# A whole transformer block on one core: inputs modulated straight from PSUM, token loads in one queue, decays behind the norms, and another order into and out of the expert loop

## The chip, the cores and the metric

One of the eight cores of a Trainium2 chip runs the program. The metric is the device time of one execution in microseconds (us), as the median of several runs. The engines named below are PE (matrix products), DVE and ACT (vector work), POOL (vector work and gathers) and SP (starts transfers). PSUM is the memory into which PE writes, SBUF the one from which it reads.

## The reference, cut to what matters

```python
h    = modulate(rmsnorm(x, g_mix), sh1, sc1)          # 512 tokens; hc likewise for 256 context tokens
proj = h @ w_in                                       # pools, q, k, v, gates, merge gates
y    = bidir_retention(q, k, v, log_sigmoid(decay), s_f, s_b)
x    = x + g1 * mix_tokens(proj, y)
hf   = modulate(rmsnorm(x, g_ffn), sh2, sc2)
# expert layer: 8 heads each choose 16 of 16384 single-neuron experts per token
g, eidx = softmax(top16), indices                     # from two top-16 lists of 128 keys
act  = gelu(einsum('thkd,td->thk', u[eidx], hf))
x    = x + g2 * einsum('thk,thkd->td', g * act, v[eidx])
out  = rmsnorm(x, final_g)
```

`modulate(h, shift, scale)` is `h * (1 + scale) + shift`; shift and scale come from products of `silu(c)` with `ada_w`.

## The kernel before, in words

Products with full float32 accuracy are made as three products of rounded parts (`mm3`): an operand is split into `hi` (a cast, on ACT, L164 or L146) and `lo` (value minus `hi`, on DVE, L169 or L147). Weights land in `raw` tiles (three buffers) and are split the same way. The order of the instructions on each engine is set by a scheduler from the order of the code, the buffers of the pools and its own estimates; each engine then runs its list strictly in order.

**The front** (`front`, `mods`). Six blocks of 128 tokens (two of context, four of x) are loaded as `xb`, alternately by SP and by ACT. `decays` computes log-sigmoid of eight decay rates with an Exp and a chain of tiny DVE operations; nothing in `mods` needs its result, the attention behind it does. ACT squares the six blocks (L299), a Sqrt makes the factors `rs`, and DVE and ACT scale the blocks. `shift_scale(i)` makes shift and scale of the two column groups k = 2i and 2i+1: one row block `ada0` through PE (L321), one `ada1` through DVE (L326, multiply and sum over `crow`, twice), then a few small operations up to `m` (L341), with two PSUM buffers of the tag U. `transpose(range(8))` turns all 48 blocks of 128x128 by PE (L362) and ACT copies them to `xT` in SBUF (L363). `modulate(i)` applies scale and shift to `xT`, ACT for the context and DVE for x, and splits the result into `hc` and `hx`. `project(i)` multiplies these by the first weights: for each k six products of 256 columns (`hc`) and twelve of 512 (`hx`).

**The experts.** All 16384 experts are computed densely for three of the four token blocks (384 tokens, `NB` = 3), 128 groups of 128 experts: `up` makes `a = gelu(u . hfT)`, in two halves each (`run_up(n)` runs n halves), `weigh` multiplies `a` by the routing weights `G` (L1173) and splits it to `ph` and `pl`, `down` adds `a . v` into six PSUM banks `Y`. The fourth block is computed by gathers on POOL and sums on DVE (`acc`). 31 groups (`AHEAD`) are taken up ahead, before `Y` exists.

The routing weights are made in **the hot loop**: for 24 sets of 16 tokens DVE writes one-hot matrices (`onehots`, L1100 to L1103), PE multiplies them (L1115), ACT writes the product from PSUM into `st` (L1116), and a transfer takes `st` to `gd` in memory. Up halves fill the loop. `prep(n)` splits the group n of u. Behind the loop come two `prep`, the first two loads of v, the reads of `G` (`read`), and steps of the top-k selection for the fourth block (`tick`, some 30 small DVE operations each, with POOL between them), then `weigh(0)`, the last up halves, and the dense loop over j: weigh(j+1), split of v, `down(j)`, one `up` in three of four steps.

**The tail.** The last `LAST` = 4 groups run down block by block. `finish` (L1038 to L1047) multiplies by `g2`, adds x, squares on ACT, normalizes and stores, for the gathered block (`f0`, started inside the loop as soon as all gathers are summed) and for the three of `Y`.

## Time and profile before

| | |
|---|---|
| median of 3 runs | 1787.21 us (1786.79 to 1787.54) |
| the profiled execution | 1787.09 us, of which its span is 1785.3 us |
| busy in the span | PE 1725.4 us, DVE 1328.0 us, ACT 777.2 us, POOL 357.8 us |
| mean granted clock of PE | 0.987 of 2.4 GHz |

The span is what the profile covers; 1.8 us lie outside it. Busy shares are means over stages with different limits, so the sections below go by stage: the front up to 72 us, attention and the rest up to 670 us, the hot loop to 800 us, the hand-over from it to the dense loop to 840 us, the dense loop, and the tail from 1755 us.

### The profile page before, as it was taken

What the parts mean: (1) busy time and instruction counts of PE and PEld (TensorE: products, weight loads), DVE (VectorE), ACT (ScalarE), POOL (GpSimd) and SP (SyncE); (2) the same over time, 40 slices, a digit from 0 to 9 for tenths busy, and PEclk for the clock granted to TensorE, in tenths of its full rate; (3) what the DMA queues carried; (4) which work ended last, traced back from release to release, by engine and by line L of the source; (5) the groups of instructions that cost most, each with busy time, mean ns of one, the idle gap of its engine ahead of it and who ended that gap; (6) DMA issues with size and microseconds to landing.
All of it is one profiled execution on the core that took longest, in us unless ns stands there. A gap on an engine that the chain in (4) does not pass through costs nothing.

```text
span 1785.3 us, 26030 instructions
## 1 busy us (share of the span) xinstructions
PE 1725.4 (97%) x9882; PEld 1552.6 (87%) x9882; DVE 1328.0 (74%) x2408; ACT 777.2 (44%) x1320; POOL 357.8 (20%) x385
## 2 busy tenths in 40 slices
PE   6999999999989998997999999999999999999997
PEld 4899988888989997986889989999899998999995
DVE  7766365664468999988947788877888777888766
ACT  7443345222344347893344344443444434444343
POOL 0222230000026840004421111221111211212100
PEclk9999999999999999998999999999999999999999
DMA  8211134675332225774569989989899899989952
GB/s 321 101 48 48 60 124 128 214 250 182 111 138 77 95 81 192 273 286 143 162 239 360 334 310 321 328 308 343 309 319 331 317 333 319 315 324 314 345 188 106
DMA packets 134190, 406.13 MB, mean 227 GB/s; under 512 B 10896, under 2 KB 60336, under 8 KB 114480
## 3 DMA queue, kind: packets, MB, share of 16 engines
q1 hardware_dynamic: 111744, 243.50, 40.7%
q0 software_dynamic: 18432, 134.23, 20.1%
q10 hardware_dynamic: 3888, 26.74, 3.6%
q8 instruction: 77, 1.26, 0.3%
q14 instruction: 49, 0.40, 0.1%
HBM read 375.05 MB, written 29.38 MB: 227 GB/s over the span
## 4 chain that ended last, share of the span: by engine, by line
PE 81%; DVE 11%; issue 2%; ACT 2%; DMA 1%; POOL 0%; DVEq 0%; ACTq 0%; SPq 0%; POOLq 0%
PE ps L154 17%; PE ps L152 17%; PE ps L153 17%; PE Y L153 9%; PE Y L154 9%; PE Y L152 9%; DVE o L1103 3%; DVE lo L169 2%; DVE eq L1100 2%; PE ps L805 1%; DVE o L1101 1%; ACT hi L164 1%; DMA keys<-keys 0%; DMA raw<-uvd 0%; PE ps L693 0%
## 5 line engine op out<-in xcount | busy, mean ns | idle before, releaser
L169 DVE TENSOR_TENSOR lo<-raw,hi 128x1024 fp32r<-128x1024 f32 x297 | 365.3, 1231 | 79.9 <-ACT hi L164 77.0
L164 ACT CAST hi<-raw 128x1024 fp32r<-128x1024 f32 x332 | 343.4, 1050 | 179.0 <-DMA raw<-uvd 96.0
L152 PE MATMUL ps<-hfT,hi 128*128 128x384 f32 x1120 | 383.4, 342 | 11.8 <-ACT hi L164 10.4
L154 PE MATMUL ps<-hfT,lo 128*128 128x384 f32 x1120 | 381.7, 341 | 10.7 <-DVE lo L169 10.7
L153 PE MATMUL ps<-hfT,hi 128*128 128x384 f32 x1120 | 379.7, 339 | 1.6 <-DVE hfT L147 1.6
L152 PE MATMUL Y<-hi,ph 128*128 128x512 f32 x768 | 299.6, 390 | 3.5 <-ACT ph L146 3.0
L153 PE MATMUL Y<-lo,ph 128*128 128x512 f32 x768 | 301.5, 393 | 0.6 <-DVE lo L169 0.5
L154 PE MATMUL Y<-hi,pl 128*128 128x512 f32 x768 | 301.6, 393 | 0.1
L1011 POOL DMA_INDIRECT uv<-uv,eidx x128 | 154.3, 1206 | 638.5 <-DVE acc L1030 601.0
L152 PEld LDWEIGHTS ps<-hfT,hi 128*128 128x128 f32 x1120 | 213.8, 191 | 16.8 <-ACT hi L164 11.4
L154 PEld LDWEIGHTS ps<-hfT,lo 128*128 128x128 f32 x1120 | 213.7, 191 | 14.2 <-DVE lo L169 14.2
L153 PEld LDWEIGHTS ps<-hfT,hi 128*128 128x128 f32 x1120 | 214.1, 191 | 5.8 <-DVE hfT L147 2.0
L1138 ACT ACTIVATE a<-ps 128x384 f32<-128x384 f32 x128 | 62.9, 491 | 315.2 <-PE ps L154 311.9
L147 DVE TENSOR_TENSOR pl<-a,ph 128x384 fp32r<-128x384 f32 x128 | 70.9, 554 | 148.7 <-ACT ph L146 148.5
L152 PEld LDWEIGHTS Y<-hi,ph 128*128 128x128 f32 x768 | 144.5, 188 | 32.3 <-ACT ph L146 3.4
L154 PEld LDWEIGHTS Y<-hi,pl 128*128 128x128 f32 x768 | 144.5, 188 | 31.4 <-DVE pl L147 1.1
L153 PEld LDWEIGHTS Y<-lo,ph 128*128 128x128 f32 x768 | 144.4, 188 | 29.8 <-DVE lo L169 1.4
L1030 DVE SCALAR_TENSOR_TENSOR acc<-uv,act,acc 128x1024 f32<-128x1024 f32 x127 | 162.5, 1280 | 5.1
L1019 DVE SCALAR_TENSOR_TENSOR uv<-uv,hf 128x1024 f32<-128x1024 f32 x128 | 154.4, 1218 | 0.0
L169 POOL TENSOR_TENSOR lo<-raw,hi 128x1024 fp32r<-128x1024 f32 x35 | 85.5, 2451 | 236.7 <-ACT hi L164 226.6
L1116 ACT ACTIVATE st<-ps 128x512 f32<-128x512 f32 x96 | 91.4, 1115 | 9.7 <-PE ps L1115 8.3
L1021 ACT ACTIVATE act<-act 128x1 f32<-128x1 f32 x128 | 25.7, 201 | 145.7 <-DVE uv L1019 145.7
(287 smaller groups left out, 2870.8 us busy)
## 6 DMA issues: line engine op xcount, KB each, us to landing
raw<-uvd SPq DMA_DIRECT2D x252, 512.0 KB, 6.2
ada<-ada SPq DMA_DIRECT2D x48, 512.0 KB, 4.7
gd<-st ACTq DMA_DIRECT2D x24, 1024.0 KB, 4.8
raw<-w_in SPq DMA_DIRECT2D x44, 512.0 KB, 4.3
G<-gd SPq DMA_DIRECT2D x85, 256.0 KB, 7.0
raw<-wq SPq DMA_DIRECT2D x16, 512.0 KB, 3.9
raw<-ret_out SPq DMA_DIRECT2D x8, 512.0 KB, 4.8
raw<-w_out SPq DMA_DIRECT2D x8, 512.0 KB, 3.7
```

The lines of the kernel that those rows point to most:

```text
L147: (eng_lo or nc.vector).tensor_tensor(lo, src, hi.bitcast(F32), ALU.subtract)
L152: mm(out, a[0], b[0], start=first, stop=False)
L153: mm(out, a[0], b[1], start=False, stop=False)
L154: mm(out, a[1], b[0], start=False, stop=last)
L164: self.nc.scalar.copy(hi, raw)
L169: eng.tensor_tensor(lo, raw, hi.bitcast(F32), ALU.subtract)
L1011: self.nc.gpsimd.indirect_dma_start(out=t, out_offset=None, in_=self.I["uv"], in_offset=bass.IndirectOffsetOnAxis(ap=self.eidx[:, s:s + 1] ...
L1019: nc.vector.scalar_tensor_tensor(t[:, :D], t[:, :D], 1.0, self.hf, ALU.mult, ALU.mult, accum_out=act[:, 0:1])
L1030: nc.vector.scalar_tensor_tensor(self.acc, t[:, D:], act[:, 1:2], self.acc, ALU.mult, ALU.add)
L1103: nc.vector.tensor_tensor(wide(o2[:, r]), wide(eq), tokens(self.gq[:, r]), ALU.mult)
L1116: nc.scalar.mul(st[:, :, t:t + 4].rearrange("p m t -> p t m"), ps, 1.0 / GSCALE)
L1138: nc.scalar.activation(a, ps[:, :N], AF.Gelu)
```

## The change

1. `decays` runs behind the Sqrt step of the norms instead of ahead of `mods`.
2. All six token blocks are loaded by SP.
3. The 48 turned blocks are no longer made in one go and copied by ACT; `modulate(i)` turns the twelve that it needs into a U buffer, and its scale and shift read PSUM.
4. One up half moves from `routes` to the end of `heads`.
5. The write of `st` runs through the same elements in another order: before, it read PSUM in rows of 512 contiguous values and wrote values 64 bytes apart; now it writes four contiguous values (16 bytes) at a time and reads values 512 bytes apart.
6. The up halves of the hot loop come ahead of the one-hots of the next set, and there are 33 instead of 32 (4 in the first step, then 1, 1, 1 and from then on 2 in every third); the `prep` of two groups moves from behind the loop into its last two steps, and that of the last group ahead of `weigh(0)`. The load of v group 1 goes behind the reads of `G`.
7. The last groups are weighed up to three ahead, in ring buffers; `f0` starts behind the loop; the last downs run half by half; `finish` multiplies and adds per half.

```diff
@@ front
-            self.decays(hp)
+            self.hp = hp
...
@@ mods
-                (nc.scalar if b % 2 else nc.sync).dma_start(
+                nc.sync.dma_start(
                     xb, I["ctx"][b * P:(b + 1) * P] if b < 2 else I["x"][(b - 2) * P:(b - 1) * P])
...
             self.rstd(rs, ss, 1.0 / D)
+            self.decays(self.hp)
...
             def modulate(i):
+
                 for k in (2 * i, 2 * i + 1):
-                    for src, h, v in ((0, hcx, 1), (2, hx, 0)):
-                        n = h[0].shape[2]
-                        t = xT[:, k, src * P:src * P + n]
+                    for src, n, h, v in ((0, 2, hcx, 1), (2, 4, hx, 0)):
+                        pt = self.ps("U")
+                        for b in range(n):
+                            nc.tensor.transpose(pt[:, b * P:(b + 1) * P], xs[src + b][:, k * P:(k + 1) * P], self.ident)
+                        t = xT[:, k, src * P:(src + n) * P]
                         m, c = m1[:, 1, k, v:v + 1], m1[:, 0, k, v:v + 1]
                         if v:
-                            nc.scalar.activation(t, t, AF.Identity, scale=m, bias=c)
+                            nc.scalar.activation(t, pt[:, :n * P], AF.Identity, scale=m, bias=c)
                         else:
-                            nc.vector.tensor_scalar(t, t, m, c, ALU.mult, ALU.add)
+                            nc.vector.tensor_scalar(t, pt[:, :n * P], m, c, ALU.mult, ALU.add)
                         self.split(t, h[0][:, k], h[1][:, k])
-
-            def transpose(ks):
-                for k in ks:
-                    for b0, n in ((0, 2), (2, 4)):
-                        pt = self.ps()
-                        for b in range(n):
-                            nc.tensor.transpose(pt[:, b * P:(b + 1) * P], xs[b0 + b][:, k * P:(k + 1) * P], self.ident)
-                        nc.scalar.copy(xT[:, k, b0 * P:(b0 + n) * P], pt[:, :n * P])
...
             shift_scale(0)
-            transpose(range(8))
             modulate(0)
@@ heads, routes
-        self.run_up(5)
+        self.run_up(6)
...
-        self.run_up(3)
+        self.run_up(2)
@@ finish
-        for s, src in zip(S, parts):
+        for i, (s, src) in enumerate(zip(S, parts)):
             nc.vector.tensor_tensor(o[:, s], src, g2[:, s], ALU.mult)
-        for i, s in enumerate(S):
             nc.vector.tensor_tensor(o[:, s], o[:, s], x[:, s], ALU.add)
@@ weights
-            nc.scalar.mul(st[:, :, t:t + 4].rearrange("p m t -> p t m"), ps, 1.0 / GSCALE)
+            nc.scalar.mul(st[:, :, t:t + 4], ps.rearrange("p t m -> p m t"), 1.0 / GSCALE)
@@ experts
-            if j < P - LAST:
+            if j < P - LAST - 2:
                 ph, pl = [dp.tile([P, N], F32R, name=x, tag=x, bufs=2) for x in ("ph", "pl")]
...
-            for h in range(2):
+            for h in halves:
...
-            oh = {}
             todo = list(range(0, N, NT))
             place(0)
+            oh = self.onehots(0, hp)
             for i, t0 in enumerate(todo):
-                for n in range(len(oh), min(i + NH, len(todo))):
-                    oh[n] = self.onehots(todo[n], hp)
-                self.run_up(2 if i % 3 == 0 else 1)
-                self.weights(t0, oh[i], hp)
+                self.run_up(1 if i % 3 or i == 3 else 2 if i else 4)
+                if i >= len(todo) - 2:
+                    self.prep(self.split_to, nc.vector)
+                now = oh
+                if i + 1 < len(todo):
+                    oh = self.onehots(todo[i + 1], hp)
+                self.weights(t0, now, hp)
...
-        k = self.split_to
-        self.prep(k, nc.vector)
-        self.prep(k + 1, nc.vector)
-        for n in range(2):
-            vs[n] = load_v(n)
-        nv[1] = 2
+        self.ask(AHEAD)
+        vs[0] = load_v(0)
         read(0, 18, 22)
         read(0, 22)
+        vs[1] = load_v(1)
+        nv[1] = 2
...
         self.run_up(3)
-        self.prep(k + 2, nc.vector)
+        self.prep(self.split_to, nc.vector)
         tick()
         self.run_up(2)
         run_v(1, nc.gpsimd)
+        self.prep(self.split_to, nc.vector)
         tick()
...
-            if j + 1 < P:
-                ps[j + 1] = weigh(j + 1, nc.vector)
+            for n in (j + 1, j + 2, j + 3) if j > P - LAST - 4 else (j + 1,):
+                if n < P and n not in ps and n >= j:
+                    ps[n] = weigh(n, nc.vector)
...
-            if j > LATE + 4 and done == S:
-                if f0 is None:
-                    f0 = self.finish(0, self.acc, [self.acc[:, 0:512], self.acc[:, 512:]], fin[2], fin[0], fin[1])
-                    next(f0)
         for b in range(NB):
-            for j in range(P - LAST, P):
-                down(j, b, ps[j], vs[j])
+            for h in range(2):
+                for j in range(P - LAST, P):
+                    down(j, b, ps[j], vs[j], [h])
...
-        for b in (0, 0, 1, 1, 1, 2, 2, 2, 3, 3, 3):
+        for b in (0, 0, 0, 1, 1, 1, 2, 2, 2, 3, 3, 3):
             next(last[b], None)
```

**PE in the front, before**: the last of the 48 turned blocks (L362; `xb` is a token block), then what follows them. The first `hc` row is the first projection.

```order
L362 MATMUL ps<-ident,xb_163 128x128
L362 MATMUL ps<-ident,xb_165 128x128
L362 MATMUL ps<-ident,xb_167 128x128
L362 MATMUL ps<-ident,xb_169 128x128
L362 MATMUL ps<-ident,xb_171 128x128
L362 MATMUL ps<-ident,xb_173 128x128
L321 MATMUL ps<-ada_353,sc 2x256 x4
L152 MATMUL ps<-hc_127,hi 128x256
L152 MATMUL ps<-hx_117,hi 128x512
```

The same place in the change (L352 turns blocks, L322 is `ada0`, L336 the small turn of its result).

```order
L352 MATMUL ps<-ident,xb_131 128x128
L352 MATMUL ps<-ident,xb_133 128x128
L352 MATMUL ps<-ident,xb_123 128x128
L352 MATMUL ps<-ident,xb_125 128x128
L152 MATMUL ps<-hc_87,hi 128x256
L153 MATMUL ps<-hc_88,hi 128x256
L154 MATMUL ps<-hc_87,lo 128x256
L352 MATMUL ps<-ident,xb_127 128x128
L352 MATMUL ps<-ident,xb_129 128x128
L352 MATMUL ps<-ident,xb_131 128x128
L352 MATMUL ps<-ident,xb_133 128x128
L152 MATMUL ps<-hc_87,hi 128x256
```

Before, all turning and the `ada` products of i = 0 and 1 stood ahead of the first projection. Now eight turned blocks stand ahead of it, four stand behind its first three products, and the `ada` products of i = 1 follow (the next two rows, not shown); the other 36 blocks stand in three groups of twelve among the projections.

**DVE in the front, before**: from the sums over `ada1` (L326; `x2` is two such rows) to the scaling of the token blocks; the small `m` rows end in L341.

```order
L326 SCALAR_TENSOR_TENSOR junk,m_161<-ada_209,crow 128x1024 x2
L326 SCALAR_TENSOR_TENSOR junk,m_161<-ada_221,crow 128x1024 x2
L190 TENSOR_SCALAR rs<-ss 128x6
L337 COPY m_161<-ps 128x4
L339 TENSOR_TENSOR m_161<-m_161,cols 128x4 x2
L341 SCALAR_TENSOR_TENSOR m_161<-m_161,cols 128x4
L169 TENSOR_TENSOR lo<-raw,hi 128x1024
L192 RECIPROCAL rs<-rs 128x6
L303 TENSOR_SCALAR xb_165<-xb_165,rs 128x1024
L303 TENSOR_SCALAR xb_169<-xb_169,rs 128x1024
```

The change has these and the tiny rows of `decays` (`lg_`) in one list. Twelve rows of it, from behind the first seven rows that need its Exp:

```order
L327 SCALAR_TENSOR_TENSOR junk,m_121<-ada_209,crow 128x1024
L192 RECIPROCAL rs<-rs 128x6
L264 TENSOR_TENSOR lg_e<-lg_e,lg_z_154 128x8
L327 SCALAR_TENSOR_TENSOR junk,m_121<-ada_209,crow 128x1024
L265 TENSOR_SCALAR lg_e<-lg_e 128x8
L304 TENSOR_SCALAR xb_125<-xb_125,rs 128x1024
L264 TENSOR_TENSOR lg_e<-lg_e,lg_z_154 128x8
L304 TENSOR_SCALAR xb_129<-xb_129,rs 128x1024
L265 TENSOR_SCALAR lg_e<-lg_e 128x8
L304 TENSOR_SCALAR xb_133<-xb_133,rs 128x1024
L264 TENSOR_TENSOR lg_e<-lg_e,lg_z_154 128x8
L327 SCALAR_TENSOR_TENSOR junk,m_121<-ada_221,crow 128x1024
```

`m` of the first two column groups (L342 now) stands behind seven more rows of `decays`, two more sums and two `lo`. Before, all of `decays` stood ahead of the first sum.

**DVE from the hot loop into the hand-over, before**: the last one-hots (L1100 to L1103), three `lo`, and the first selection rows.

```order
L1100 TENSOR_TENSOR eq<-ioh,ig 128x2048
L1101 TENSOR_TENSOR o_8218<-ioh,ig 128x2048
L1103 TENSOR_TENSOR o_8220<-eq,ig 128x2048 x2
L169 TENSOR_TENSOR lo<-raw,hi 128x1024 x3
L945 MAX sv_8366<-s_4764 128x8 x2
L947 MAX_INDEX si_8367<-sv_8366,s_4764 128x8 x2
L950 MATCH_REPLACE s_4764<-sv_8366,s_4764 128x128 x2
L945 MAX sv_8366<-s_4764 128x8 x2
```

The same place in the change (L1094 to L1097 are the one-hots).

```order
L1097 TENSOR_TENSOR o_8174<-eq,ig 128x2048 x2
L169 TENSOR_TENSOR lo<-raw,hi 128x1024
L1094 TENSOR_TENSOR eq<-ioh,ig 128x2048
L1095 TENSOR_TENSOR o_8241<-ioh,ig 128x2048
L1097 TENSOR_TENSOR o_8243<-eq,ig 128x2048 x2
L169 TENSOR_TENSOR lo<-raw,hi 128x1024
L940 MAX sv_8363<-s_4748 128x8 x2
L942 MAX_INDEX si_8364<-sv_8363,s_4748 128x8 x2
L945 MATCH_REPLACE s_4748<-sv_8363,s_4748 128x128 x2
```

Two of the three `lo` that stood behind the last one-hots now stand between one-hots; one is left behind them.

## Rows read from the trace of the kernel before

**Rows 1.** The page: busy time by engine, and the chain that ended last.

```profile
PE 1725.4 (97%) x9882; PEld 1552.6 (87%) x9882; DVE 1328.0 (74%) x2408; ACT 777.2 (44%) x1320; POOL 357.8 (20%) x385
...
PE 81%; DVE 11%; issue 2%; ACT 2%; DMA 1%; POOL 0%; DVEq 0%; ACTq 0%; SPq 0%; POOLq 0%
```

**Rows 2.** Windows: stretch, length, busy by engine, granted clock, DMA share, GB/s.

```profile
20.00:30.00 10.00, 7.51 (x44) 4.54 (x45) 9.60 (x21) 9.96 (x17) 0.00 (x0) 0.83 0.91 356
35.00:72.00 37.00, 36.98 (x182) 26.50 (x182) 24.80 (x55) 17.94 (x34) 4.66 (x2) 1.00 0.48 168
680.00:800.00 120.00, 111.31 (x1080) 104.64 (x1081) 118.59 (x104) 103.52 (x117) 0.00 (x0) 0.96 0.73 269
806.00:846.00 40.00, 30.37 (x134) 27.48 (x135) 34.50 (x144) 11.91 (x17) 19.84 (x61) 0.83 0.43 139
```

**Rows 3.** Timeline of PE in the front: start, length, instruction, idle before.

```profile
25.63 6.39 PE L362 MATMUL ps<-ident,xb 128*128 128x128 f32 x48
31.94 1.89 PE L321 MATMUL ps<-ada,sc 128*2 128x256 f32 x8
...
34.92 0.39 PE L152 MATMUL ps<-hc,hi 128*128 128x256 f32 x1 [1.09 <-ACT hc L146]
...
42.58 3.62 PE L321 MATMUL ps<-ada,sc 128*2 128x256 f32 x16
...
72.02 0.39 PE L152 MATMUL ps<-hi,hc 128*128 128x256 f32 x1
```

**Rows 4.** Timeline of ACT in the front.

```profile
8.94 0.21 ACT L257 ACTIVATE lg_e<-lg_e 128x8 f32<-128x8 f32 x1 [1.72 <-DVE lg_e L256]
...
9.83 1.06 ACT L299 ACTIVATE junka<-xb 128x1024 f32<-128x1024 f32 x1
...
10.89 1.54 ACT L202 COPY crow<-ps 128x512 f32<-128x512 f32 x3
...
21.83 1.28 ACT L191 ACT_TABLE_LOAD   x1
```

**Rows 5.** Timeline of DVE in the front.

```profile
9.18 0.17 DVE L258 TENSOR_SCALAR lg_z<-lg_e 128x8 f32<-128x8 f32 x1 [0.27 <-ACT lg_e L257]
...
14.46 0.16 DVE L273 TENSOR_SCALAR lc<-lg 128x4 f32<-128x4 f32 x1
...
17.66 1.23 DVE L326 SCALAR_TENSOR_TENSOR junk<-ada,crow 128x1024 f32<-128x1024 f32 x1
...
21.80 0.16 DVE L341 SCALAR_TENSOR_TENSOR m<-m,cols 128x4 f32<-128x4 f32 x1
21.88 1.23 DVE L169 TENSOR_TENSOR lo<-raw,hi 128x1024 fp32r<-128x1024 f32 x1
...
23.59 2.08 DVE L303 TENSOR_SCALAR xb<-xb,rs 128x1024 f32<-128x1024 f32 x3
```

**Rows 6.** Groups by form on ACT: out<-in xcount | busy, mean ns | idle before.

```profile
L1116 ACT ACTIVATE st<-ps 128x512 f32<-128x512 f32 x96 | 91.4, 1115 | 9.7 <-PE ps L1115 8.3 <-DMA gd<-st 1.4
...
L618 ACT ACTIVATE gt<-ps 128x512 f32<-128x512 f32 x16 | 9.5, 595 | 23.2 <-PE ps L154 23.2
```

**Rows 7.** Timeline of DVE from the end of the hot loop on.

```profile
806.72 2.36 DVE L169 TENSOR_TENSOR lo<-raw,hi 128x1024 fp32r<-128x1024 f32 x2 [7.89 <-ACT hi L164]
...
826.96 1.47 DVE L1173 TENSOR_TENSOR a<-a,G 128x384 f32<-128x384 f32 x3
...
857.55 1.21 DVE L169 TENSOR_TENSOR lo<-raw,hi 128x1024 fp32r<-128x1024 f32 x1
```

**Rows 8.** Timeline of PE in the hand-over.

```profile
829.41 0.69 PE L152 MATMUL ps<-hfT,hi 128*128 128x384 f32 x1 [7.42 <-ACT hi L164]
```

**Rows 9.** Timeline of PE and DVE in the tail.

```profile
1759.27 0.50 PE L152 MATMUL Y<-hi,ph 128*128 128x512 f32 x1 [2.96 <-ACT ph L146]
...
1765.52 1.28 DVE L1038 TENSOR_TENSOR od<-Y,uv 128x512 f32<-128x512 f32 x2
...
1780.53 1.41 DVE L1047 SCALAR_TENSOR_TENSOR od<-od,ss,uv 128x512 f32<-128x512 f32 x2
```

More of the change, by code (lines that the diff above doesn't have):

```diff
@@ L1184, in weigh, with down @@
             return ph, pl
-        def down(j, b, p, v):
+        def down(j, b, p, v, halves=(0, 1)):
             pb = [x[:, b * P:(b + 1) * P] for x in p]
-            for h in range(2):
+            for h in halves:
                 s = slice(h * 512, (h + 1) * 512)
@@ L1249, in goal @@
             return min(P, AHEAD + (j + 1) * (P - AHEAD) // JE)
-        f0 = None
         for j in range(P):
@@ L1313, in experts @@
                 nc.sync.dma_start(fin[2 + b], self.xd[b * P:(b + 1) * P])
-            if j > LATE + 4 and done == S:
-                if f0 is None:
-                    f0 = self.finish(0, self.acc, [self.acc[:, 0:512], self.acc[:, 512:]], fin[2], fin[0], fin[1])
-                    next(f0)
         for b in range(NB):
-            for j in range(P - LAST, P):
-                down(j, b, ps[j], vs[j])
+            for h in range(2):
+                for j in range(P - LAST, P):
+                    down(j, b, ps[j], vs[j], [h])
         assert not live and fetched == S
-        last = [f0] + [self.finish(1 + b, self.wp.tile([P, D], F32, name="od", tag="raw", bufs=NRAW), Y[b],
+        last = [self.finish(0, self.acc, [self.acc[:, 0:512], self.acc[:, 512:]], fin[2], fin[0], fin[1])] + [self.finish(1 + b, self.wp.tile([P, D], F32, name="od", tag="raw", bufs=NRAW), Y[b],
                                    fin[3 + b], fin[0], fin[1]) for b in range(NB)]
-        for b in (0, 0, 1, 1, 1, 2, 2, 2, 3, 3, 3):
+        for b in (0, 0, 0, 1, 1, 1, 2, 2, 2, 3, 3, 3):
             next(last[b], None)
```

## The prediction, made before the change was run

> **What bounds the kernel now.** I read the page first: PE is busy 97% of the span and the chain that ended last lies 81% on PE and 11% on DVE [rows 1]. A change can win only where PE waits or runs at half clock, or in a stretch that DVE bounds; any PE work that is put into a full stretch is paid in full. So I went by windows. In the front PE has gaps and a granted clock of 0.83 up to 30 us, but from the first projection on it is full: 36.98 of 37 us from 35 to 72 [rows 2]. In the hot loop DVE is the bound, 118.6 of 120 us, with ACT at 103.5 and PE at 111.3. From 806 to 846 PE is busy only 30.4 of 40 us, at a clock of 0.83 [rows 2]: the hand-over to the dense loop. The timelines of these places gave the rest.
>
> **Front.** Before, everything that PE does besides projecting stood ahead of the first projection at 34.92: 48 turned blocks in 6.39 us, 0.133 each, and the `ada` products of i = 0 and 1; those of i = 2 and 3, 3.62 us each, lie among the projections, which end at 72.02 [rows 3]. After, by the order of instructions, 8 turned blocks stand ahead and 40 behind (40 x 0.133 = 5.3 us), and the `ada` products of i = 1 stand behind too (3.6 us). The projections did not wait for anything, so this is +8.9 us on PE. The 16 copies on ACT that go away freed ACT, not PE.
>
> When does the first projection start? Before, ACT idled 1.72 us ahead of the Exp at 8.94 and squared from 9.83 [rows 4]. Without Exp and its table load ahead ACT is free at 8.94 - 1.72 - 1.28 = 5.9. Six squares at 1.06 and four copies at 1.54/3 are 8.4 us, so they end near 14.5 if the tokens are there (one queue issues them earlier than the block that stood behind the Exp). Table load and Exp: 16.2 [rows 4]. Now DVE has `decays` on the way to `m`. The 29 rows from 9.18 to 14.46 took 5.3 us, 0.18 each, as a chain; seven stand alone in front of the first sum (1.3 us), twelve more stand between long rows, where I take 0.1 each (`m` at 21.80 and the next row at 21.88) [rows 5]. With five sums (1.25 each), two `lo` (1.2 each), three scalings (2.1) and 0.7 for the rows of `m`, DVE needs 1.3 + 1.2 + 6.3 + 2.4 + 2.1 + 0.7 = 14.0 us and `m` comes at about 30.5, where it came at 21.80 [rows 5]. That is late: until now `m` waited for the copies, now ACT's scaling and cast wait for `m`. With 1.3 us for these the first projection starts at 31.8, 3.1 us earlier than before.
>
> Two prices remain. Only two U buffers pass the turned blocks, and each must be read before PE may go on; I follow the first group and three later ones and find about 1.3 us of waits on PE (row by row, from 0.1 to 0.8 each; bounds 0 and 4). And PE now stands almost idle from about 16 to 32 us, so it starts the full stretch at the lower level: before, ten us with waits were granted 0.83 [rows 2], which is 1.7 us of clock, and I take that (bounds 0 and 2.7). Front: -3.1 + 8.9 + 1.3 + 1.7 = **+8.8 us** (bounds +4, where `m` comes 2 us earlier and neither price is paid, and +12). Nothing behind it gives this back: PE goes straight on at 72.02 [rows 3].
>
> **One half up earlier.** It fills a PE wait of about 2 us ahead of the hot loop, but DVE has its own rows there until the one-hots; I count 0 (bounds 0 and -2).
>
> **Other order of the eviction.** It takes 1.115 us, 96 times [rows 6]. A contiguous read and write of the same size on ACT takes 0.595 [rows 6]. The new form writes in runs of 16 bytes but reads PSUM in steps of 512 bytes, and no row shows such a read. Below: 0.6 us. Above: no row bounds it; twice the old form's excess would be 1.6 us. I take a value between 0.6 and 1.1, nearest to the contiguous row. It is worth 0 in the loop, because DVE is the bound [rows 2]; the cover is ACT's free 16.5 us in 120, or 0.18 us for each of some 90 evictions, so it costs nothing up to about 1.3 us.
>
> The Trainium skill speaks on both sides of this edit (Advanced Engine Details and Errata, Memory Cachelines): in SBUF an access pattern wants at least two hits on a 16-byte line, which the new write gives and the old did not, while in PSUM, with lines of 8 bytes, non-contiguous patterns are called slow. By its first half the eviction falls to about 0.6 us and the time stays; by its second half it is the slow rival below. The old form's 1.115 against 0.595 agrees with the first half; no run here shows the second.
>
> **Hand-over.** Before, DVE stood idle 7.89 us after the last one-hots, waiting for two casts that ACT had queued behind the last evictions; then came two `lo` (2.36 us) and the selection, up to `a` times `G` at 826.96 [rows 7]. PE idled 7.42 us until 829.41, because the cast of the last group stood on ACT behind `ph` of weigh(0) [rows 8]; that group then ran at the lower clock. Now two more `lo` stand between one-hots, on the bounding engine (their 2.36 us are moved, not saved), one is left behind, which I let wait 1.3 us for its cast, and the last group is split ahead of weigh(0), so PE runs through. DVE gains 7.9 - 1.3 = 6.6 us, and about 2 us of short waits after 829, all on casts of ACT that hung behind PE's late last halves: 8.6. PE gains more: its 7.42 and the clock, 0.17 of 40 us [rows 2], 14.2 in all. But the first downs need `pl` and the split v from DVE, which is full of selection steps until the `lo` at 857.55 [rows 7], and there PE waits for DVE before and after. So DVE's gain counts: **-8.5 us** (bounds -4, if the cast waits behind four evictions of 1.1 us again, and -14.2).
>
> **Tail.** PE waited 2.96 us for `ph`, which stood on ACT behind the square of `f0` [rows 9]. Weighing ahead removes this. But the end hangs on DVE: three finishes of 5.47 us, from 1765.52 to 1781.94 [rows 9]. Now `f0` runs wholly behind the last `lo`, near 1757.5: four products and sums 2.5, square 1.3, table load 1.3, root 0.5, scaling 1.4, so the first finish of `Y` starts at 1764.5, 1.0 earlier; overlapping the squares gives 0.2 more for each. **-1.6 us** (bounds 0 and -3).
>
> **Sum.** +8.8 + 0 + 0 - 8.5 - 1.6 = -1.3 against the profiled 1787.09 (its span and 1.8 us around it), which lies 0.12 below the median: **1785.8 us**, no change that this kernel's measurement can tell (0.2%, 3.6 us, either way).
>
> **Rivals.**
> - *The hand-over gives PE's whole gain.* If the selection steps let `pl` and v through in time, the gain is 14.2 instead of 8.5: 1787.1 + 8.8 - 14.2 - 1.6 = 1780.1. For it: PE's idle time is that large. Against it: DVE is busy 34.5 of those 40 us [rows 2]. A front at its lower bound would end near the same time, 1781. Faster.
> - *The eviction becomes the bound* (the other side). Place: ACT in the hot loop. From about 1.3 us on each further 0.1 us costs 96 x 0.1 = 9.6 us; at 1.4 us the time is 1785.8 + 9.6 = 1795, at 1.6 us 1815. For it: a read in steps that no row shows; against it: writing four values together takes away what made the old form dear.
> - *The cast is late again.* The one `lo` behind the last one-hots waits for ACT behind four evictions (4 x 1.1 us): hand-over -4, 1790.3; with the front a little dearer it is measurably slower.
> - *The front costs nothing.* With `m` as early as 21.80 again the first projection would start near 23, and -11.9 + 8.9 + 1.3 would be -1.7 instead of +8.8: 1775.3. This needs `decays` to be free on DVE; the order of the list speaks against it, and I give it no chance of its own.
>
> **How the numbers follow.** My forecast 0.38; the first rival (with the cheap front) 0.36; the late cast 0.14; the slow eviction 0.12. Faster takes the first rival, 0.36; the late cast splits 0.04 and 0.10 between same and slower; so same is 0.38 + 0.04 = 0.42 and slower 0.10 + 0.12 = 0.22. The range leaves out the slow eviction (0.12) and some 0.08 of both outer ends: 1779.5 to 1792. My own forecast alone would span 1783 to 1789.
>
> **What would show it.** Front: first projection near 32 us and its end near 81 us instead of 72.02, with 40 turned blocks after the first. Eviction: mean between 0.6 and 1.1 us, DVE still full from 680 to 800. Hand-over: no idle of 7.4 us on PE, the first `down` some 15 us earlier than before relative to the hot loop's end, and DVE's fourth v `lo` 8 to 9 us earlier relative to it. Tail: no wait of PE for `ph`. I am wrong if the front ends before 77 or after 84 us, if PE does not wait for DVE in the first downs, or if an eviction takes over 1.3 us.

## The result, and the profile after

The change is slower. Its median is 1797.83 us (four runs, 1796.56 to 1799.45) against 1787.38 us of the kernel before beside it (four runs, 1786.79 to 1787.97): a ratio of 1.0057, 95% interval 1.0044 to 1.0070, so 10.4 us lost. The forecast was 1785.8 us, no measurable change, and the range ended at 1792.0. The profiled execution took 1797.56 us with a span of 1795.8 us, 10.5 us more than before.

By place, the windows of the change that answer to [rows 2] (stretch, length, busy time of PE, of its weight loads, of DVE, ACT and POOL, granted clock, DMA share, GB/s):

```profile
35.00:79.00 44.00, 42.68 (x218) 30.22 (x217) 26.96 (x54) 15.86 (x28) 4.90 (x2) 1.00 0.47 165
680.00:800.00 120.00, 102.77 (x1010) 96.35 (x1009) 115.51 (x102) 64.31 (x112) 0.00 (x0) 0.99 0.67 251
814.00:854.00 40.00, 33.36 (x185) 30.61 (x183) 33.29 (x150) 12.45 (x19) 20.71 (x64) 0.96 0.40 137
```

The hand-over does what was asked of PE (33.4 busy of 40 us instead of 30.4, clock 0.96 instead of 0.83), but in the hot loop DVE, the bound, is no longer full: 115.5 of 120 us instead of 118.6. (The loop starts later in the change; from 689 to 809 us, as far into it as before, DVE is busy 115.3 us.)

PE in the front, in the timeline of the change, to be set against [rows 3]:

```profile
26.79 0.85 PE L352 MATMUL ps<-ident,xb 128*128 128x128 f32 x3
28.82 0.69 PE L352 MATMUL ps<-ident,xb 128*128 128x128 f32 x2 [1.18 <-ACT xT L356]
...
31.51 4.67 PE L322 MATMUL ps<-ada,sc 128*2 128x256 f32 x16
...
58.18 0.88 PE L352 MATMUL ps<-ident,xb 128*128 128x128 f32 x6 [0.71 <-ACT xT L356]
...
79.49 0.28 PE L152 MATMUL ps<-hi,hc 128*128 128x256 f32 x1
```

The turned blocks and the `ada` products now stand between projections, with waits for the U buffers. The first sixteen `ada` products among them take 4.67 us instead of 3.62; the granted clock was 0.67 from 20 to 30 us and 0.82 from 30 to 40. The projections end at 79.49 instead of 72.02 us, **7.5 us later**. `m` came at 27.94, the first projection at 29.25.

The eviction, in the groups by form on ACT, beside the contiguous one of the same size, as in [rows 6]:

```profile
L1110 ACT ACTIVATE st<-ps 128x512 f32<-128x512 f32 x96 | 49.6, 604 | 29.1 <-PE ps L1109 27.1 <-DMA gd<-st 1.8
...
L613 ACT ACTIVATE gt<-ps 128x512 f32<-128x512 f32 x16 | 9.5, 593 | 23.2 <-PE ps L154 23.2
```

It fell from 1115 to 604 ns, nearly as cheap as a contiguous one.

The start of the hot loop, in the timeline of DVE:

```profile
679.39 1.23 DVE L1094 TENSOR_TENSOR eq<-ioh,ig 128x2048 f16<-128x2048 f16 x1
...
683.94 2.35 DVE L169 TENSOR_TENSOR lo<-raw,hi 128x1024 fp32r<-128x1024 f32 x2
...
695.09 1.23 DVE L169 TENSOR_TENSOR lo<-raw,hi 128x1024 fp32r<-128x1024 f32 x1 [4.26 <-ACT hi L164]
```

What stands there on PE, and then on ACT:

```profile
685.22 0.44 PE L154 MATMUL ps<-hfT,lo 128*128 128x384 f32 x1 [4.76 <-DVE lo L169]
...
690.74 1.46 PE L1109 MATMUL ps<-o,o 128*128 128x128 f16 x23
```

```profile
691.53 2.07 ACT L1110 ACTIVATE st<-ps 128x512 f32<-128x512 f32 x4
693.63 0.34 ACTq L1111 DMA_DIRECT2D gd<-st  x1
694.01 1.05 ACT L164 CAST hi<-raw 128x1024 fp32r<-128x1024 f32 x1 [0.42 <-ACT st L1110]
```

A ring of waits is read off here. PE has four up halves to run ahead of the first one-hot products and stands 4.76 us for a `lo` that DVE has behind the first one-hots; so the one-hot products start at 690.74, the evictions end at 693.6, the cast behind them runs at 694.01, and DVE, which needs that cast for its next `lo`, stands 4.26 us. The last one-hots start at 811.03, 131.6 us behind the first, where it was 124.8.

In the hand-over (DVE, then PE; compare [rows 7] and [rows 8]):

```profile
813.30 1.22 DVE L169 TENSOR_TENSOR lo<-raw,hi 128x1024 fp32r<-128x1024 f32 x1
814.44 0.48 DVE L940 MAX8 sv<-s 128x8 f32<-128x128 f32 x2
...
823.13 1.23 DVE L169 TENSOR_TENSOR lo<-raw,hi 128x1024 fp32r<-128x1024 f32 x1 [3.92 <-ACT hi L164]
...
837.38 1.47 DVE L1167 TENSOR_TENSOR a<-a,G 128x384 f32<-128x384 f32 x3
```

```profile
839.28 0.80 PE L152 MATMUL Y<-hi,ph 128*128 128x512 f32 x1 [4.98 <-ACT a L1132]
```

The wait of 7.89 us behind the loop is gone: the one `lo` that is left there, at 813.30, waits for nothing. But 3.92 us have come back at the next `lo`, between selection steps, and PE still stands 4.98 us ahead of the first `down`.

In the tail (compare [rows 9]), first two rows of before, three casts on ACT and the last `lo` on DVE, then ACT, PE and DVE of the change:

```profile
1743.44 2.95 ACT L164 CAST hi<-raw 128x1024 fp32r<-128x1024 f32 x3
1760.20 1.22 DVE L169 TENSOR_TENSOR lo<-raw,hi 128x1024 fp32r<-128x1024 f32 x1 [0.40 <-ACT hi L164]
```

```profile
1749.64 0.49 ACT L1132 ACTIVATE a<-ps 128x384 f32<-128x384 f32 x1 [6.46 <-PE ps L154]
1750.03 0.92 ACT L146 CAST ph<-a 128x384 fp32r<-128x384 f32 x2
1752.09 0.51 ACT L146 CAST ph<-a 128x384 fp32r<-128x384 f32 x1 [1.15 <-DVE a L1167]
1752.51 2.94 ACT L164 CAST hi<-raw 128x1024 fp32r<-128x1024 f32 x3
```

```profile
1767.58 0.75 PE L152 MATMUL Y<-hi,ph 128*128 128x512 f32 x1 [1.23 <-ACT hi L164]
1768.84 0.79 PE L153 MATMUL Y<-lo,ph 128*128 128x512 f32 x1 [0.51 <-DVE lo L169]
```

```profile
1767.56 1.23 DVE L169 TENSOR_TENSOR lo<-raw,hi 128x1024 fp32r<-128x1024 f32 x1 [0.39 <-ACT hi L164]
1768.70 0.68 DVE L1033 TENSOR_TENSOR acc<-acc,uv 128x512 f32<-128x512 f32 x1
...
1775.27 0.68 DVE L1033 TENSOR_TENSOR od<-Y,uv 128x512 f32<-128x512 f32 x1
1775.99 0.69 DVE L1034 TENSOR_TENSOR od<-od,uv 128x512 f32<-128x512 f32 x1
1776.60 0.68 DVE L1033 TENSOR_TENSOR od<-Y,uv 128x512 f32<-128x512 f32 x1
...
1780.95 0.68 DVE L1033 TENSOR_TENSOR od<-Y,uv 128x512 f32<-128x512 f32 x1
```

PE no longer waits for `ph`, it waits for casts of v instead. The casts stand on ACT behind three `ph`, and the first of those behind a gelu that waits for PE. Less the 7.0 us by which the dense loop is late, the three casts come 2.0 us later than before. What ends last is DVE: `f0` starts only at 1768.70, behind the last `lo`, the first finish of `Y` at 1775.27, and a finish takes 5.68 us where it took 5.43. PE's last product starts at 1785.72, ahead of the third finish at 1786.63.

The same marks for every kernel run show which place an edit touches. All are start times out of the timelines: the front's end (PE); the first one-hots; the way from the first to the last one-hots and from these to the first MAX (DVE); `pl` of the eleventh group (DVE), against 905.42 before, whose distance then stays within 0.1 us up to group 122; and the tail, which is the change of the span less that distance.

| kernel | front's end | hot loop starts | loop | to MAX | dense loop | tail | span |
|---|---|---|---|---|---|---|---|
| before | 72.02 | 670.51 | 124.8 | 13.7 | 0 | 0 | 1785.3 |
| the change | 79.49 | 679.39 | 131.6 | 3.4 | +7.0 | +3.5 | 1795.8 |
| e1 | 71.19 | 669.01 | 132.5 | 3.4 | -2.5 | +2.6 | 1785.4 |
| e2 | 79.68 | 679.87 | 124.7 | 10.2 | +4.9 | +3.5 | 1793.7 |
| e3 | 79.38 | 679.06 | 131.7 | 3.4 | +6.7 | 0.0 | 1792.0 |
| e4 | 73.19 | 672.10 | 124.8 | 11.8 | 0.0 | +0.1 | 1785.4 |
| e5 | 71.47 | 670.05 | 124.9 | 13.9 | -0.3 | +0.1 | 1785.1 |
| e6 | 77.98 | 677.07 | 125.4 | 13.9 | +6.3 | 0.0 | 1791.6 |
| e7 | 72.90 | 671.30 | 127.1 | 3.4 | -7.0 | +0.2 | 1778.5 |
| e8 | 71.61 | 669.27 | 132.6 | 3.4 | -2.2 | 0.0 | 1783.1 |
| e9 | 71.74 | 669.50 | 126.1 | 13.4 | -1.1 | +1.9 | 1786.1 |
| e10 | 71.95 | 670.68 | 125.3 | 14.0 | +1.4 | +2.0 | 1788.7 |
| e11 | 72.63 | 670.56 | 127.1 | 3.4 | -5.9 | +2.2 | 1781.6 |
| e12 | 79.25 | 678.87 | 127.4 | 3.4 | +0.8 | +3.5 | 1789.6 |
| e13 | 80.61 | 680.21 | 143.9 | 3.4 | +21.8 | +3.2 | 1810.3 |
| e14 | 72.87 | 671.25 | 124.8 | 11.8 | -2.1 | 0.0 | 1783.2 |

For the change this adds up: the hot loop starts 8.9 us late (7.5 of the front, 1.4 of the attention behind it), the way from there into the dense loop gives back 1.9, the tail takes 3.5; together 10.5. The 1.9 are a sum of four: the loop is 6.8 us longer (4.5 of waits for casts, the rest the two `lo` that moved into it), the way from the last one-hots to the first MAX 10.2 shorter, from there to the first `a` times `G` 5.0 longer, and from that to `pl` of the eleventh group 3.4 shorter.

### The profile page after: what moved, and what is told of

Its sections match the earlier page's. It is cut to its first block, busy times and chain, and to the rows that moved or that the text cites. A ratio compares the mean times of both kernels' runs of the same rounds, so it can differ in the third digit from the quotient of the medians.

```text
span 1795.8 us, 26010 instructions
## 1 busy us (share of the span) xinstructions
PE 1728.0 (96%) x9882; PEld 1551.0 (86%) x9882; DVE 1329.7 (74%) x2408; ACT 733.3 (41%) x1304; POOL 359.1 (20%) x385
## 4 chain that ended last, share of the span: by engine, by line
PE 50%; DVE 9%; issue 1%; ACT 1%; DMA 0%; POOL 0%; DVEq 0%; ACTq 0%; POOLq 0%
PE Y L153 9%; PE Y L154 9%; PE Y L152 9%; PE ps L154 8%; PE ps L152 8%; PE ps L153 8%; DVE o L1097 3%; DVE lo L169 1%; DVE eq L1094 1%; DVE o L1095 0%; ACT hi L164 0%; DMA raw<-uvd 0%; PE ps L1109 0%; DVE od L1034 0%; DVE si L942 0%
## 5 line engine op out<-in xcount | busy, mean ns | idle before, releaser
L153 PEld LDWEIGHTS ps<-hfT,hi 128*128 128x128 f32 x1120 | 211.7, 189 | 5.9 <-DVE hfT L147 2.1
L152 PEld LDWEIGHTS ps<-hfT,hi 128*128 128x128 f32 x1120 | 211.8, 189 | 5.6 <-ACT hfT L146 1.7
L152 PE MATMUL ps<-hx,hi 128*128 128x512 f32 x224 | 88.4, 396 | 1.1 <-ACT yTt L597 1.1
L154 PE MATMUL ps<-hx,lo 128*128 128x512 f32 x224 | 88.6, 395 | 0.0
```

The costliest lines, as they stand in the source:

```text
L152: mm(out, a[0], b[0], start=first, stop=False)
L153: mm(out, a[0], b[1], start=False, stop=False)
L154: mm(out, a[1], b[0], start=False, stop=last)
```

## The experiments

Kernels whose front is as before reach the hot loop between 669.0 and 672.1 us (the table), and the front's end varies from 71.2 to 73.2 among them; so a single trace is read place by place, relative to the loop's start, and what an edit is worth is told by the medians.

### The front: e1, e5, e6

**e1**, the change without its edits 1 to 3.

```diff
             self.rstd(rs, ss, 1.0 / D)
-            self.decays(self.hp)
...
+            transpose(range(8))
             modulate(0)
```

(and the scaling from `xT` and the loads by two queues, as before).

> The change with its front (parts 1, 2 and 3) put back. Theory S, the sum of places: matching instructions of the two traces stand 9.5 us later at 660 us, 7.0 us later in the steady dense loop and 10.5 us later at the end, so the front and the attention behind it cost 9.5 us, the hot loop and the hand-over give back 2.5, the tail costs 3.5, and each place stands for itself: about 1788.3 us here. Rival: most of the front's delay is swallowed later or the later losses need the front; then 1792 us or more.

Measured: 1787.56 us, ratio 0.9999 (0.9990 to 1.0008). Theory S holds, within 0.8 us. The front is as large as the whole loss; the other edits together are worth nothing.

**e5**, the kernel before with edits 1 and 2 alone.

```diff
-                (nc.scalar if b % 2 else nc.sync).dma_start(
+                nc.sync.dma_start(
...
             self.rstd(rs, ss, 1.0 / D)
+            self.decays(self.hp)
```

> The kernel before with edits 1 and 2 alone (decays behind the Sqrt step, all token loads by SP); the turned blocks go through ACT's copies as before. Theory M (the front's loss is the 40 turned blocks and the ada products that now lie behind the first projection; an m that comes late costs nothing as long as the copies run anyway): first projection no later than 34.9 us, front's end 69 to 72 us, time 1785 to 1788, ratio 0.998 to 1.000. Rival D (the tiny rows of decays on DVE are the loss, as they stand ahead of m): first projection 3 to 6 us later than 34.92, time 1790 to 1794, ratio 1.002 to 1.004.

Measured: 1788.42 us, ratio 1.0002 (0.9993 to 1.0011). The first projection came at 31.14, 3.8 us earlier, but the front's end only 0.6 us: behind it PE waits 1.86 us for a `lo` of `hx` on DVE at 56.40, and the granted clock of that stretch is 0.96 where it was 1.00. The places are M's, the time lies 0.4 us above its range. Rival D falls for these edits alone: the tiny rows of `decays` in DVE's list cost nothing that can be measured. Beside edit 3 it was not tested.

**e6**, the kernel before with edit 3 alone.

```diff
-                            nc.scalar.activation(t, t, AF.Identity, scale=m, bias=c)
+                            nc.scalar.activation(t, pt[:, :n * P], AF.Identity, scale=m, bias=c)
...
-            transpose(range(8))
             modulate(0)
```

> The kernel before with edit 3 alone (modulated inputs straight from PSUM). Theory M: m comes at 21.8 us as before, so the first projection can start near 25 to 27 us, some 8 to 10 us earlier, and PE pays the 8.9 us of turned blocks and ada products behind it and 1 to 2 us of waits for the two U buffers: front's end 72 to 74 us, time 1786.5 to 1790, ratio 1.000 to 1.0015. Rival D says the same of this kernel and puts the 7.5 us of the whole change on decays alone. Rival U (U buffers and the reads of PSUM on DVE cost far more than 2 us): front's end 77 us or later, time over 1791.

Measured: 1795.79 us, ratio 1.0044 (1.0031 to 1.0058), beyond what theory M gave it. Edit 3 carries the loss. Time and front's end (77.98) are those that rival U gave, but its cause is not there: PE's waits for the two U buffers are 1.6 us in all (0.33, 0.22, 0.16, 0.71, 0.22), as M had them. What M had too large is the head start. The first projection starts at 27.95, 7.0 us earlier and not 8 to 10. PE runs only one product there before it waits for the scaling on ACT, and the stretch begins at a low clock (granted 0.56 in the mean from 20 to 30 us, that is mostly the lower level of 1.2 of 2.4 GHz, and 0.81 from 27.95 to 37.00). From the first projection to the front's end it takes 50.0 us instead of 37.1: 8.9 of moved work, 1.6 of waits for the U buffers and 2.4 that are left, of which the clock up to 37.00 is some 1.7 (an estimate: 0.19 of 9.05 us). In the kernels with the whole front of the change the front ends at 79.3 to 80.6, another 1.3 to 2.6 us later; whether edits 1 and 2 cost this beside edit 3 no run shows.

### The hot loop and the hand-over: e2, e4, e14, e13, e8, e7, e12

**e2**, the change without edits 4 and 6 (the evictions keep their new order).

```diff
+            oh = {}
...
-            oh = self.onehots(0, hp)
             for i, t0 in enumerate(todo):
-                self.run_up(1 if i % 3 or i == 3 else 2 if i else 4)
...
+                self.run_up(2 if i % 3 == 0 else 1)
```

> The change with the up half, the hot loop and the hand-over (parts 4 and 6) put back, the new eviction kept. Theory S: what these parts give is lost again, and only the eviction's own gain stays (0 to 3 us): 1797.5 to 1800.4 us. Rival L: the new loop is a loss by itself (DVE waits 4.3 us for a cast behind the first eviction, and 3.9 us later on): 1796 us or less.

Measured: 1797.45 us, ratio 1.0052 (1.0039 to 1.0066): the same as the change, between the two expectations (0.05 us below S). The new order of the loop, which should have been the main gain, gives nothing as it stands.

**e4** and **e14**, the kernel before with the evictions' order alone, twice.

```diff
-            nc.scalar.mul(st[:, :, t:t + 4].rearrange("p m t -> p t m"), ps, 1.0 / GSCALE)
+            nc.scalar.mul(st[:, :, t:t + 4], ps.rearrange("p t m -> p m t"), 1.0 / GSCALE)
```

> The kernel before with the other order of the eviction (part 5) alone. Theory S: DVE bounds the loop, so nothing there; behind it the two lo wait for casts that stand behind the last evictions, and those are four times 0.5 us shorter: 1785 to 1786 us, DVE's 7.89 us of waiting down to about 6. Rival: no change at all, 1787.4 us, because the dense loop's start is set by PE's late last up.

> The kernel before with the evictions' order alone, once more. Theory E: median 1783 to 1786, ratio 0.997 to 0.9985, the loop as long as before and the first MAX 1.5 to 2.5 us earlier behind the last one-hots. Rival N: 1786.5 to 1788.5; the 4.3 us of the first measurement were chance.

Measured: 1783.79 us, ratio 0.9975 (0.9966 to 0.9984), and 1783.93 us, 0.9978 (0.9969 to 0.9987). The loop is as long as before, as DVE bounds it; the gain is behind it, where the casts stand behind evictions: DVE waits 6.00 us there (e14: 6.04) instead of 7.89, and the first MAX comes 11.8 instead of 13.7 us behind the last one-hots. The two measurements agree, so rival N falls. From the loop's start to the dense loop the traces show 1.6 us (e4) and 2.8 us (e14); the medians say 3.7 to 4.3. The rest is not seen in these two traces, and both are of executions slower than their median (1787.19 and 1785.03 us).

**e13**, the change with the evictions in their old order (the diff above, backwards).

> The whole change with the evictions in their old order. Theory E (the shorter evictions free ACT, so the casts behind them are earlier and DVE's lo with them; worth 2 to 4 us): 1800 to 1803, ratio 1.0065 to 1.0085, first MAX at least 1.5 us later than in the change relative to the loop's start. Rival N (the edit is worth nothing, as DVE bounds the loop): 1796.5 to 1799, ratio 1.005 to 1.006.

Measured: 1811.89 us, ratio 1.0131 (1.0115 to 1.0146). Inside the change the edit is worth 14 us, far more than theory E gave it. The groups on DVE in the loop show where, first for e13 (680 to 824 us), then for the change (680 to 812):

```profile
L169 DVE TENSOR_TENSOR lo<-raw,hi 128x1024 fp32r<-128x1024 f32 x17 | 20.7, 1222 | 16.2 <-ACT hi L164 16.2
```

```profile
L169 DVE TENSOR_TENSOR lo<-raw,hi 128x1024 fp32r<-128x1024 f32 x17 | 20.7, 1222 | 4.5 <-ACT hi L164 4.5
```

In the new order the casts stand on ACT behind four evictions. At 1.12 us each DVE waits 6.51 us for the first and 1.2 to 1.3 us for seven more; at 0.60 us little but the first wait (4.26) is left. The two edits belong together.

**e8**, the kernel before with the evictions' order and edits 4 and 6; **e7** the same with two halves in the first step. From e8 to e7 one line changes:

```diff
-                self.run_up(1 if i % 3 or i == 3 else 2 if i else 4)
+                self.run_up(1 if i % 3 else 2)
```

> The kernel before with the evictions' order and edits 4 and 6 as the change has them (4 up halves in the first step); front and tail as before. Theory H: time 1785 to 1788, so the hand-over gives nothing beyond the eviction's gain (1783.8 with the eviction alone), hot loop some 6 us longer than with the eviction alone. Rival W: the same time, but the loss lies behind the loop, in DVE's waits for casts between selection steps: the loop is as long as with the eviction alone plus 2.4 us, and the first MAX comes as late as in the change relative to the last one-hots.

> The kernel before with the evictions' order and with edits 4 and 6, but with 2 up halves in the first step of the hot loop where the change has 4 (and 1 instead of 2 in no other step). Theory H (in the change DVE stood 4 to 5 us in the first steps, since four halves ahead of the first products put the casts and the evictions behind PE's up work): hot loop 4 us shorter than in the change, last one-hots 126 to 129 us behind the loop's start where the change needed 132; time 3 to 5 us below the kernel with 4 halves that runs beside this. Rival W (the stall is only moved, because DVE's lo must wait for a cast in any case or because the two halves less are missing later in the hand-over): the two kernels agree within 1.5 us.

Measured: e8 1785.60 us, ratio 0.9986 (0.9977 to 0.9995); e7 1781.73 us, 0.9964 (0.9950 to 0.9977). One line, with two halves fewer in the first step and one more in the fourth, is worth 3.9 us. In e8 DVE stands 5.17 us for a cast in the second step, in e7 it doesn't, and the loop is 5.5 us shorter. The rows of DVE in e8:

```profile
678.36 2.35 DVE L1103 TENSOR_TENSOR o<-eq,ig 128x2048 f16<-128x2048 f16 x2
685.88 1.23 DVE L169 TENSOR_TENSOR lo<-raw,hi 128x1024 fp32r<-128x1024 f32 x1 [5.17 <-ACT hi L164]
```

and the same two rows in e7:

```profile
679.25 2.35 DVE L1103 TENSOR_TENSOR o<-eq,ig 128x2048 f16<-128x2048 f16 x2
681.52 1.22 DVE L169 TENSOR_TENSOR lo<-raw,hi 128x1024 fp32r<-128x1024 f32 x1
```

Theory H holds (only e8's loop, 7.8 us longer than e4's, is beyond the 6 it gave); rival W, that the stall only moves, falls. With two halves the way from the loop's start into the dense loop is 7.8 us shorter than before (0.8 later at the loop, 7.0 earlier behind it).

**e12**, the whole change with that one line.

> The whole change, but with 2 up halves instead of 4 in the first step of the hot loop (and 2 in the fourth, so that 32 run in all). Theory H: the loss of the hand-over is these halves: the hot loop is 126 to 128 us long instead of 131.6, and the dense loop starts 4 to 6 us earlier than in the change: time 1791 to 1794, ratio 1.002 to 1.0035. Rival W (the later front lets other things decide, for example the casts behind the last evictions): the gain is under 2 us, time over 1795.5.

Measured: 1793.82 us, ratio 1.0032 (1.0020 to 1.0043), 4.0 us under the change. The loop is 127.4 us long, DVE's waits for casts in it are 0.2 us instead of 4.5, and the way into the dense loop is 7.5 us shorter than before (in a trace of an execution 2.4 us under its median). The same line decides with either front.

### The tail: e3, e9, e10

**e3**, the change without edit 7 (its diff is longer; the part on the weighing).

```diff
-            for n in (j + 1, j + 2, j + 3) if j > P - LAST - 4 else (j + 1,):
-                if n < P and n not in ps and n >= j:
-                    ps[n] = weigh(n, nc.vector)
+            if j + 1 < P:
+                ps[j + 1] = weigh(j + 1, nc.vector)
```

> The change with its tail (part 7) put back. Theory S: the tail costs 3.5 us, so 1794.3 us. Rival: the late tail only follows from the loads' place after the hand-over, and the tail of before would be as late: 1797.8 us.

Measured: 1794.62 us, ratio 1.0043 (1.0030 to 1.0057): edit 7 costs 3.2 us by the medians, 3.5 by the traces.

**e9**, the kernel before with the weighing ahead alone (the diff above, backwards, and the ring buffers).

> The kernel before with the weighing ahead of edit 7 alone (up to three groups ahead, in ring buffers); downs, f0 and finish as before. Theory A (three ph stand on ACT ahead of the casts of the last v, so the loads of the last v go out some 8 us late and the last downs wait for them): the 2.96 us wait of PE for ph is gone, but PE's last product comes 1.5 to 3 us later, time 1789.5 to 1791.5, ratio 1.001 to 1.002. Rival F (the tail's loss lies in f0 behind the loop and in the finishes half by half): time 1784 to 1788, no loss here.

Measured: 1789.51 us, ratio 1.0007 (0.9998 to 1.0015). The median alone does not decide; the trace has a tail that is 1.9 us longer. PE of e9 there:

```profile
1746.78 0.50 PE L153 MATMUL Y<-lo,ph 128*128 128x512 f32 x1 [0.77 <-DVE lo L169]
...
1761.24 0.60 PE L152 MATMUL Y<-hi,ph 128*128 128x512 f32 x1 [1.83 <-ACT hi L164]
1762.50 0.79 PE L153 MATMUL Y<-lo,ph 128*128 128x512 f32 x1 [0.66 <-DVE lo L169]
```

The 2.96 us for `ph` are gone and 3.26 us for `hi` and `lo` have come: another operand of the same products is late. These waits alone are only 0.3 us more than before. The larger part of the 1.9 us is PE's clock behind them; the windows from 1760 to 1770 us, first before, then e9:

```profile
1760.00:1770.00 10.00, 9.93 (x37) 7.45 (x37) 7.78 (x17) 4.12 (x10) 0.00 (x0) 0.83 0.14 52
1760.00:1770.00 10.00, 8.10 (x22) 6.11 (x23) 7.86 (x16) 4.21 (x9) 0.00 (x0) 0.66 0.14 52
```

The granted clock is 0.66 instead of 0.83, some 1.7 us (an estimate: 0.17 of 10 us); products stand 0.43 us apart up to 1768.2 where at the full clock they stand 0.23 apart, PE's last product comes 2.0 us later relative to the dense loop, and the second finish on DVE waits 1.48 us for PE. The place is theory A's, but the last loads of v go out only 2.0 us later (relative to the dense loop) and not 8.

**e10**, the kernel before with the rest of edit 7.

```diff
-            if j > LATE + 4 and done == S:
-                if f0 is None:
-                    f0 = self.finish(0, self.acc, [self.acc[:, 0:512], self.acc[:, 512:]], fin[2], fin[0], fin[1])
-                    next(f0)
...
-                down(j, b, ps[j], vs[j])
...
+                    down(j, b, ps[j], vs[j], [h])
```

> The kernel before with the rest of edit 7 (f0 behind the loop, the last downs half by half, finish per half), weighing as before. Theory A: PE's end as before, distance from PE's last product to the end within 1 us of before, time 1786.5 to 1789. Rival F: the distance from PE's last product to the end grows by 1.5 us or more, or the first finish of Y starts later than 1765.5 because f0 stands ahead of it on DVE: time 1790 to 1792.

Measured: 1789.85 us in eleven executions (a twelfth, of 6102 us, is left out), ratio 1.0012 (1.0004 to 1.0021). PE's last product stands at 1777.45, 0.3 us earlier than before if the 1.3 us are taken off by which this execution's dense loop was late, but the way from there to the end grew by 2.4 us: rival F by its signs, with a time just under its range. The finishes on DVE set it, since `f0` stands ahead of them (first finish of `Y` at 1768.20) and each takes 5.68 us instead of 5.43.

### The best of it: e11

The kernel of e7 with the downs half by half and the finish per half.

> The kernel with the evictions' order and edits 4 and 6 with 2 halves in the first step (1781.7 where it ran before), and of edit 7 only the downs half by half and the finish per half; f0 and the weighing as before the change. If the last block's first half is finished while PE works on its second, the end comes 1 to 2 us closer to PE's last product: 1779.5 to 1781, ratio 0.995 to 0.996. If the three finishes hang on DVE's pitch and not on PE, nothing is gained: 1781 to 1782.5.

Measured: 1782.19 us, ratio 0.9966 (0.9953 to 0.9979): no better than e7, as the second expectation had it, with a tail 2.2 us longer in the trace. There the first finish of `Y` waits for PE between its halves: their multiplies start at 1759.94 and 1762.44, 2.5 us apart instead of 1.3 as in e10. e7 stays the fastest kernel of the study, 0.36% under before.

## Why the prediction was wrong

The sum was +8.8 (front) + 0 (half moved) + 0 (eviction) - 8.5 (hand-over) - 1.6 (tail) = -1.3. The trace has +8.9, -1.9 and +3.5, which is 10.5. Two terms failed.

**Front: right in mechanism, and in size partly by luck.** It is 7.5 us at the front's own end (forecast 8.8, and 81 for the end that came at 79.5); the 8.9 at the start of the hot loop fit only because another 1.4 us came behind the front, which the forecast did not have. `m` and the first projection came 2.6 us earlier than worked out (0.3 of this is a slip: the terms 16.2 and 14.0 add up to 30.2 and not to 30.5). Behind it the moved work is the 8.9 us, the waits for the U buffers are 1.3 us as forecast (0.22, 0.16, 0.71, 0.22), and 2.9 us are left for the clock and the rest, where 1.7 stood. The 1.4 us are not explained: from the front's end to the hot loop the kernels with the change's front take 599.6 to 600.2 us, those with the front of before 597.7 to 598.9. Nor are the 2 us by which the losses alone (7.6 of e6, 3.2 of e3) and the gain of e8 (2.6) fall short of the change's 10.4.

**Hand-over: the step that failed is the one on the loop.** "Two more `lo` stand between one-hots, on the bounding engine" was priced at what they take, 2.36 us, and the first step's four halves at nothing, with DVE "still full from 680 to 800". The halves ahead of the first products delay the evictions, these the cast, and the cast DVE: 4.3 us. Behind the loop the one `lo` that was given 1.3 us waited for nothing, but the next one, to which the prediction gave no wait, stood 3.92 us for a cast behind a gelu that waited for PE. So 1.9 us came of 8.5. The mechanism itself was right: with two halves first it gave 7.5 to 7.8 us in the traces (e12, e7), beside the forecast 8.5; 1.6 to 2.8 us of this is the eviction's (e4, e14). The first `down` did come 13.9 us earlier relative to the last one-hots (forecast some 15), but PE's own 14.2 us, the first rival, never came of it; PE waits for DVE and ACT in the first downs, as the prediction said.

**Eviction: right in length, wrong in worth.** 0.604 us lies at the lower bound. That it shortens no loop that DVE bounds is right (124.8 us in e4 and e14); that it is worth 0 is not, as the hand-over's casts stand behind evictions: 3.7 to 4.3 us alone and 14 us in the new order. The cover "ACT's free 16.5 us in 120" was a mean; what counts is the four evictions ahead of each cast.

By the Trainium skill (Advanced Engine Details and Errata, Memory Cachelines) at least two hits on a 16-byte line of SBUF are needed to absorb the access latency, and in PSUM non-contiguous patterns slow down matmuls and two neighbours should lie together. The first agrees with 1115 falling to 604 ns; the second, which the prediction stretched to a read by ACT, does not show in one in steps of 512 bytes, at 604 against 593 ns contiguous. So the slow eviction, the rival on the losing side, fell.

**Tail: the sign was wrong.** The wait for `ph` did go, but the prediction did not ask what else those products need: casts of v, now behind three `ph`. It also let `f0` start near 1757.5, behind a last `lo` for whose time it has no row. Before, that `lo` stood at 1760.20; in the change it came at 1767.56, 0.3 us later than before when the 7.0 us are taken off by which the dense loop was late. So `f0` started at 1768.70 and put the first finish of `Y` at 1775.27, 3.8 us behind the forecast 1764.5 even with the 7.0 us added, and 2.7 us later than before. And "overlapping the squares gives 0.2 more for each" was 0.25 us the other way: multiply and add of one half stand back to back, each waiting for the one before it, and the second half's square starts no earlier behind the last sum; the three finishes make the other 0.7 us. This is the chain that ends the change. In e9, where `f0` stands as before, PE's waits and its clock behind them set the end (1.9 us), so the two halves of edit 7 lose in different ways (1.9 and 2.0 us, together 3.5).

The range failed as both wrong terms lay on one side (6.6 and 5.1 us), and no rival had the tail as a loss.

## What to carry to other kernels

When work is moved ahead in an in-order list, follow the ring of engines through the first step and not through the steady state: PE's list delays ACT's, ACT's delays the cast, and the cast stops the bounding engine. A shorter operation off the critical path is worth what stands behind it in its queue, and that can be much more in another order (14 us against 4), so edits are to be priced in pairs. Before a wait at the end is taken away, look which of the other operands of the same products is next late, and what granted clock the products behind the new waits get.

## What the runs showed of the hardware

ACT reads 512 values per partition from PSUM in steps of 512 bytes nearly as fast as in a row (604 and 593 ns), if it writes four at a time. On DVE two rows of 512 values start 0.72 us apart where the second needs the first's result (a multiply at 1775.27, its add at 1775.99), and 0.61 us where it does not (that add, and the next multiply at 1776.60).
